# Thirteenth paired unit for the queries and forget gates of heads 4 and 5, bias table and key-value norm moved into the index stage, three attentions beside the branch projection

## The chip, the cores and the metric

One NeuronCore of one Trainium2 chip runs the whole kernel. The metric is device time in microseconds of one execution; three runs give the median. The engines are PE (TensorE, matrix products), DVE (VectorE), ACT (ScalarE), POOL (GpSimd) and SP (SyncE, which here issues nearly all DMAs). Each engine executes its own instructions in the order in which the program emits them, and waits at an instruction until its inputs are there; everything behind it on that engine waits too.

## The reference

One layer on x of shape (1, 512, 2048) in float32. Cut to what matters:

```
h    = rmsnorm(x)
a_q, a_f, a_i, a_g, c_q, c_kv, k_idx, w_idx, b_g, m_a, m_b = split(h @ w_in)
# branch A, 8 heads of 128: gated linear recurrence over chunks
q = silu(a_q) * 128**-0.5 ; f = lb + (1 - lb) * sigmoid(a_f) ; k = 1 - f ; v = a_i
y_a = rmsnorm(recurrence(q, k, log f, v)) * silu(a_g)
# branch B, 8 heads of 128: an indexer picks 128 keys for each query
cq = rmsnorm(c_q);  q = cq @ w_uq;  k, v = rmsnorm(c_kv) @ w_ukv
score = sum_h relu((cq @ w_qidx)_h . layernorm(k_idx)) * w_idx_h, visible keys only
sel = top_k(score, 128)
y_b = softmax(q k[sel] / sqrt(128) + bias_table[t5_bucket(sel - t)]) v[sel] * silu(b_g)
merged = sigmoid(m_a) * (y_a @ w_pa) + sigmoid(m_b) * (y_b @ w_pb)
out = rmsnorm(x + merged @ w_out)
```

## The kernel before

All matrix products are made of three products of float32r halves (`mm3`, lines 76 to 78): high by high, high by low, low by high. So each block of weights that comes in by DMA (`wr`, 128 x 1024 words, 512 KB) is first split into a high half by ACT (`wh`, L72) and a low half by DVE (`wl`, L73). `prep(i)` does that two blocks ahead of the block that PE works on, and issues the loads further ahead.

There are two kinds of projection jobs. A plain job (`feat_job`) makes one product for each block of 128 features, with 512 columns. A paired unit (`pair_job`, `pair_unit`) takes 512 output features and works by the Winograd form of Strassen's rule: seven products of half size where eight would be needed, with 256 columns each, on sums of inputs and of weights made beforehand (`pair_sums`, L145 to L154). A unit is 8 steps of 7 x 2 x 3 = 42 matrix products, 336 in all. Twelve units run one after the other early on: eleven for gates, and one for the queries and forget gates of heads 6 and 7, which it leaves in DRAM (`qf_d`).

The program is written as one list of jobs. Small work is put into generators, one queue ("lane") for each kind: `hgrn` (the recurrence of two heads, `hgrn_gen(p)` for heads 2p and 2p+1), `top` (the selection), `att` (attention of two heads, `att_gen(p)`), `norm`, `misc`, `t5` (the bias table). `pump()` is called between pieces of a projection job, and advances the first generator of each lane by one `yield`. So the order of the instructions on every engine is fixed by hand: by how many pumps lie between one step of a generator and the next. In a plain job over two blocks of features a pump follows each 12 matrix products of 512 columns. `late` is a list of DMA stores and other calls; what is put there is issued by the `flush` two pumps later.

The order of the stages around the change is: the twelve units; `open_branches`, which loads what the later stages need from DRAM; the index stage (eight jobs on `w_qidx`, each two index heads, with the relu'd scores summed into `M`); `end_index`, which starts `hgrn_gen(3)`, `t5_gen` and `norm_gen` of the key-value rank; `ai_job(3)` (values of heads 6, 7); `af_aq(0)`, `ai_job(1)`, `af_aq(1)`, `ai_job(2)` (forget gates and queries as plain jobs, values), with the selection beside them; `uqkv(0)` (queries, keys, values of attention 0); `af_aq(2)` with attention 0 beside it; `uqkv(1)`; a last plain gate job with attention 1 and the recurrence of heads 4, 5; `uqkv(2)`; the branch projection on `w_pa`, eight plain jobs, with attention 2 beside the first four; `uqkv(3)`; attention 3 beside the last four; then `w_pb`, and the output.

`t5_gen` sets `rb` to zero on POOL and loads `rb`, the one-hot table `oh` and `flip`, two pumps later multiplies `rb` by `oh` on PE (L465), stores the differences in DRAM from ACT's queue, reads them back in a skewed pattern, flips them on PE (L478), and stores the bias of each head in DRAM (`bh_d`), again from ACT's queue. `norm_gen` squares `ckv` on ACT, sums the squares on PE (L575, L576 through L81), takes logarithm and exponential on ACT, and scales and splits the two rows.

`att_gen` loads the bias and adds it to the selection mask on POOL (`att_bias`, `MB`), two pumps later makes the scores (`att_scores`: PE, then DVE adds and takes maxima, two pumps later ACT's exponentials and DVE's scaling), three pumps later transposes them on PE (`att_turn`), and two pumps later multiplies by the values (`att_values`).

Of the kernel before, what the change touches and what calls it, by code (L numbers as in the profile page):

```python
# [34 lines left out]
T, D = 512, 2048  # L35
# [7 lines left out]

STILL, MOVED, RANK = 16, 48, 48

# [5 lines left out]
def hybrid_block(ctx, tc, x, norm_w, w_in, lb_table, gnorm_a, q_norm_w, kv_norm_w, w_uq,  # L51
# [50 lines left out]
    cq_d = dram.tile([4, 128, T], F32, name="cq_d")  # L102
    qf_d = dram.tile([2, 2, 128, T], F32, name="qf_d")

# [103 lines left out]

    def feat_job(src, col, ntile, nk, kc, rhs, evac, before=None, width=T, after=None, place=0):
        at = len(specs)  # L210
        n = ntile * 128
        for k in range(0, nk, kc):
            specs.append(([(0, n, src[k * 128:(k + kc) * 128, col:col + n])], kc, n, place))

        def run():
            if before:
                before()
            ps = [mmp.tile([128, T], F32, name="acc")[:, 0:width] for _ in range(ntile)]
            for i in range(nk // kc):
                prep(at + i)  # L220
                wh, wl = halves.pop(at + i)
                for c in range(ntile):
                    for k in range(kc):
                        kk = i * kc + k
                        rh, rl = rhs(kk)
                        s = slice(c * 128, c * 128 + 128)
                        mm3(ps[c], wh[:, k, s], wl[:, k, s], rh, rl, kk == 0, kk == nk - 1)
                    if kk == nk - 1:
                        evac(c, ps[c])
                    if ntile < 4 or c % 2:  # L230
                        pump()
                if after and i in after:
                    after[i]()

        jobs.append(run)
# [197 lines left out]
    def open_branches():  # L433
# [12 lines left out]
        R.i = enter("norms")  # L446
        R.last = [R.i.tile([128, 2, T], F32, name=n) for n in ("hf", "hk", "hq")]
        R.ckv = R.i.tile([128, 2, T], F32, name="ckv")
        for t, src in ((R.last[0], qf_d[1]), (R.last[2], qf_d[0]), (R.ckv, ckv_d)):
            SP.dma_start(t, src.rearrange("f p t -> p f t"))  # L450

    def t5_gen():
# [108 lines left out]
    def norm_gen(raw, n, w, hi, lo):  # L561
# [16 lines left out]
        yield  # L578
        for j in range(n):
            t = R.i.tile([128, T], F32, name="nt", bufs=2)  # L580
            V.scalar_tensor_tensor(t, raw[:, j, :], w[:, j:j + 1], r, op0=OP.mult, op1=OP.mult)
            split(hi[:, j, :], lo[:, j, :], t)
            if j % 2:
                yield

# [66 lines left out]

    def ai_job(p):
# [25 lines left out]
    def af_evac(p):  # L681
        def evac(c, ps):
            if c == 0:
                if p:
                    drain("hgrn")
                hg[p, "f"] = R.h.tile([128, 2, T], F32, name="hf")
                hg[p, "k"] = R.h.tile([128, 2, T], F32, name="hk")
            f, k, h = hg[p, "f"][:, c, :], hg[p, "k"][:, c, :], 2 * p + c
# [5 lines left out]
    def aq_evac(p):  # L694
        def evac(c, ps):
            if c == 0:
                hg[p, "q"] = R.h.tile([128, 2, T], F32, name="hq")
            q = hg[p, "q"][:, c, :]
# [6 lines left out]
    def hgrn_gen(p):  # L705
        f, k, q = R.last if p == 3 else (hg[p, n] for n in "fkq")

        def place(shape, dtype, name, tag):
            pool = R.i if p == 3 and tag in ("hf", "hk", "hq") else R.h
            return pool.tile(shape, dtype, name=name, tag=tag)  # L710

        gate = R.h.tile([128, 2, T], F32, name="hg")
# [5 lines left out]
        qf, kf, tot = (a.rearrange("p c t -> p (c t)") for a in (q, k, f))  # L718
        if p == 3:
            for c in range(2):  # L720
                V.tensor_scalar(f[:, c], f[:, c], oml[:, 6 + c:7 + c], lb[:, 6 + c:7 + c], op0=OP.mult, op1=OP.add)
            V.tensor_scalar(k, f, -1.0, 1.0, op0=OP.mult, op1=OP.add)
# [67 lines left out]
        yield  # L790
        sq = place([128, 2, T], F32, "hk", "hk")
        zs = []
        o = place([128, 2, T], F32, "ho", "hf")
        for c in range(2):
# [8 lines left out]
            yield  # L803
            zs.append((place([128, T], FR, "hzh", ("hkd", "hst")[c]), place([128, T], FR, "hzl", ("hq", "hS")[c])))
            split(*zs[c], sq[:, c])
# [12 lines left out]
        for c in range(2):  # L818
            y = [place([128, T], FR, f"hy{i}", (("hkd", "hst"), ("hq", "hS"))[i][c]) for i in range(2)]
            split(*y, sq[:, c])  # L820
# [127 lines left out]

    def att_gen(p):
        MB = att_bias(2 * p)  # L950
# [9 lines left out]
        yield  # L960
        att_values(p, 0, PT)
        P = yield from att_scores(p, 1, MB)
        yield
        yield
        yield
        PT = att_turn(P)
        yield
        yield
        att_values(p, 1, PT)
# [164 lines left out]
    def end_index():  # L1134
# [4 lines left out]
        R.h = enter("hgrn", side="right")  # L1139
        lanes["hgrn"].append(hgrn_gen(3))  # L1140
        lanes["t5"].append(t5_gen())
        lanes["norm"].append(norm_gen(R.ckv, 2, c_kvw, R.ckh, R.ckl))

    def open_att():
        drain("norm")
        drain("t5")
        leave("norms")
        R.a = enter("att")
# [37 lines left out]
    def end_hgrn():  # L1186
# [4 lines left out]
        R.u = enter("us", side="right")  # L1191
        load_y(R.ya, ya_d, 4, 6)

    gate_job(44, {1: lambda: (take_x(R.ya, 0), load_y(R.ya, ya_d, 0, 4)),
                  3: lambda: (take_x(R.ya, 1), load_y(R.ya, ya_d, 6, 8)),
                  6: end_hgrn, 7: lambda: take_x(R.yb, 2)})
# [3 lines left out]

    uqkv(2)
    jobs.append(lambda: load_y(R.yb, yb_d, 0, 4))

# [292 lines left out]
```

## Time and profile before

| | |
|---|---|
| median of 3 runs | 1380.72 us (1380.17 to 1382.21) |
| profiled execution | 1380.42 us, of which 1378.6 us are the span from its first to its last instruction |
| PE busy | 1357.1 us, 98% |
| DVE busy | 1062.2 us, 77% |
| ACT busy | 625.0 us, 45% |
| POOL busy | 82.6 us, 6% |
| DMA | 201.59 MB, mean 146 GB/s |
| granted TensorE clock | 0.998 of full speed |

Busy time of PE is modelled from pipelined matrix products, whose records overlap, so it hides small waits. The distance from the start of one matrix product to the start of the next is the surer measure: a stage's duration over its count of products. Times in rows count from the start of the span.

### The profile page before, as it was taken

What the parts mean: (1) busy time and instruction counts of PE and PEld (TensorE: products, weight loads), DVE (VectorE), ACT (ScalarE), POOL (GpSimd) and SP (SyncE); (2) the same over time, 40 slices, a digit from 0 to 9 for tenths busy, and PEclk for the clock granted to TensorE, in tenths of its full rate; (3) what the DMA queues carried; (4) which work ended last, traced back from release to release, by engine and by line L of the source; (5) the groups of instructions that cost most, each with busy time, mean ns of one, the idle gap of its engine ahead of it and who ended that gap; (6) DMA issues with size and microseconds to landing.
All of it is one profiled execution on the core that took longest, in us unless ns stands there. A gap on an engine that the chain in (4) does not pass through costs nothing.

```text
span 1378.6 us, 26386 instructions
## 1 busy us (share of the span) xinstructions
PE 1357.1 (98%) x10796; PEld 1250.5 (91%) x10796; DVE 1062.2 (77%) x1744; ACT 625.0 (45%) x986; POOL 82.6 (6%) x85
## 2 busy tenths in 40 slices
PE   8999999999999999999999999999999999999997
PEld 7888999999999999999878889888888888899996
DVE  6796889988888888777759698667555558899856
ACT  5555445545444444466252433543643333454434
POOL 2100000000000000000302012103010100000000
PEclk9999999999999999999999999999999999999999
DMA  6335345544444444443325243344494656643564
GB/s 205 92 102 143 104 142 169 153 138 140 146 144 129 115 140 138 151 151 94 92 79 155 62 139 89 119 126 148 155 314 159 222 161 215 212 147 121 162 205 169
DMA packets 141834, 201.59 MB, mean 146 GB/s; under 512 B 10209, under 2 KB 83602, under 8 KB 141586
## 3 DMA queue, kind: packets, MB, share of 16 engines
q1 hardware_dynamic: 140322, 198.53, 46.4%
q8 instruction: 84, 1.38, 0.4%
q10 hardware_dynamic: 1392, 1.39, 0.3%
q14 instruction: 36, 0.29, 0.1%
HBM read 165.80 MB, written 34.09 MB: 145 GB/s over the span
## 4 chain that ended last, share of the span: by engine, by line
PE 86%; DVE 9%; ACT 2%; issue 1%; DMA 1%; POOL 0%; ACTq 0%; SPq 0%; DVEq 0%; POOLq 0%
PE pp L77 14%; PE pp L76 14%; PE pp L78 14%; PE acc L76 12%; PE acc L78 12%; PE acc L77 12%; DVE wl L73 1%; PE acc L81 1%; PE hl L81 1%; DVE M L648 1%; DVE m L647 1%; PE ho L81 1%; DVE hq L744 1%; PE sc L78 1%; PE sc L76 1%
## 5 line engine op out<-in xcount | busy, mean ns | idle before, releaser
L150 ACT ACTIVATE bh<-wr 128x768 fp32r<-128x768 f32 x120 | 101.5, 846 | 209.4 <-issue 116.7
L72 ACT ACTIVATE wh<-wr 128x1024 fp32r<-128x1024 f32 (+1 forms) x112 | 116.5, 1042 | 166.0 <-PE acc L77 59.1
L73 DVE TENSOR_TENSOR wl<-wr,wh 128x1024 fp32r<-128x1024 f32 (+1 forms) x112 | 137.7, 1230 | 66.2 <-ACT wh L72 66.2
L152 ACT ACTIVATE wh<-sv 128x512 fp32r<-128x512 f32 x240 | 141.9, 622 | 78.3 <-DVE sv L145 60.2
L78 PE MATMUL pp<-sh,wl 128*128 128x256 f32 x576 | 159.5, 277 | 0.0
L76 PE MATMUL pp<-sh,wh 128*128 128x256 f32 x576 | 159.5, 277 | 0.0
L77 PE MATMUL pp<-sl,wh 128*128 128x256 f32 x576 | 159.4, 277 | 0.0
L154 DVE TENSOR_TENSOR wl<-sv,wh 128x1024 fp32r<-128x1024 f32 x120 | 146.7, 1222 | 7.1 <-ACT wh L152 1.1
L153 DVE TENSOR_TENSOR bl<-wr,bh 128x768 fp32r<-128x768 f32 x120 | 114.6, 955 | 48.2 <-ACT bh L150 47.7
L76 PE MATMUL acc<-xh,wh 128*128 128x512 f32 x368 | 148.0, 402 | 0.0
L78 PE MATMUL acc<-xh,wl 128*128 128x512 f32 x368 | 143.8, 391 | 1.5 <-DVE wl L73 1.5
L77 PE MATMUL acc<-xl,wh 128*128 128x512 f32 x368 | 143.4, 390 | 0.0
L77 PEld LDWEIGHTS pp<-sl,wh 128*128 128x128 f32 x576 | 108.3, 188 | 0.0
L78 PEld LDWEIGHTS pp<-sh,wl 128*128 128x128 f32 x576 | 108.3, 188 | 0.0
L76 PEld LDWEIGHTS pp<-sh,wh 128*128 128x128 f32 x576 | 108.3, 188 | 0.0
L76 PE MATMUL pp<-xh,bh 128*128 128x256 f32 x384 | 106.0, 276 | 0.0
L78 PE MATMUL pp<-xh,bl 128*128 128x256 f32 x384 | 106.0, 276 | 0.0
L77 PE MATMUL pp<-xl,bh 128*128 128x256 f32 x384 | 106.0, 276 | 0.0
L76 PE MATMUL acc<-yh,wh 128*128 128x512 f32 x256 | 100.0, 391 | 0.0
L78 PE MATMUL acc<-yh,wl 128*128 128x512 f32 x256 | 99.7, 389 | 0.0
L77 PE MATMUL acc<-yl,wh 128*128 128x512 f32 x256 | 99.7, 389 | 0.0
L145 DVE TENSOR_TENSOR sv<-wr 128x512 f32<-128x512 f32 x120 | 82.3, 686 | 8.6 <-DMA wr<-in_w_in_dram 5.2
(386 smaller groups left out, 3639.3 us busy)
## 6 DMA issues: line engine op xcount, KB each, us to landing
wr<-in_w_in_dram SPq DMA_DIRECT2D x144, 512.0 KB, 3.7
wr<-in_w_out_dram SPq DMA_DIRECT2D x32, 512.0 KB, 3.9
mg<-gate_d SPq DMA_DIRECT2D x48, 256.0 KB, 5.0
gate_d<-c SPq DMA_DIRECT2D x44, 256.0 KB, 4.5
wr<-in_w_pa_dram SPq DMA_DIRECT2D x16, 512.0 KB, 4.1
wr<-in_w_pb_dram SPq DMA_DIRECT2D x16, 512.0 KB, 4.2
wr<-in_w_in_dram SPq DMA_DIRECT2D x20, 256.0 KB, 2.8
x<-in_x_dram SPq DMA_DIRECT2D x8, 512.0 KB, 6.8
```

The source lines that it names most:

```text
L72: A.activation(hi, src, AF.Copy)
L73: V.tensor_tensor(lo, src, hi.bitcast(F32), op=OP.subtract)
L76: PE.matmul(ps, lh, rh, start=first, stop=False, skip_group_check=True)
L77: PE.matmul(ps, lh, rl, start=False, stop=False, skip_group_check=True)
L78: PE.matmul(ps, ll, rh, start=False, stop=last, skip_group_check=True)
L81: PE.matmul(ps, l, r, start=first, stop=last, skip_group_check=True)
L145: V.tensor_tensor(sv[:, 0:2, :], b[:, 1:3, :], b[:, 0:1, :].to_broadcast([128, 2, 256]), op=OP.add)
L150: A.activation(bh, b[:, 1:4, :], AF.Copy)
L152: A.activation(vh[:, i:i + 2, :], sv[:, i:i + 2, :], AF.Copy)
L153: V.tensor_tensor(bl, b[:, 1:4, :], bh.bitcast(F32), op=OP.subtract)
L154: V.tensor_tensor(vl, sv, vh.bitcast(F32), op=OP.subtract)
L647: V.max(m8, m)
```

## The change

It does five things. The queries and forget gates of heads 4 and 5 become a thirteenth paired unit, behind the one for heads 6 and 7; `af_aq(2)` goes away, and the results are read from DRAM (`qf_d` doubles), with scaling done in `hgrn_gen`. The recurrences run in the order 3, 2, 0, 1, with `ai_job(2)` behind `ai_job(3)`. The bias table and the key-value norm start in `open_branches`, beside the index jobs, rather than behind them; the table's stores go through `late` to SP's queue rather than ACT's, with other counts of pumps between its steps. Attention 0 runs beside the last gate job, and attentions 1, 2 and 3 beside the branch projection, which now pumps twice as often (`often`), with one more pump in each rest of those three. And the weights of `w_uq` are put 32 words lower in their buffer (`RANK`).

```
-STILL, MOVED, RANK = 16, 48, 48
+STILL, MOVED, RANK = 16, 48, 16
...
+                        if often and k == 1:
+                            pump()
...
     R.i = enter("norms")
-    R.last = [R.i.tile([128, 2, T], F32, name=n) for n in ("hf", "hk", "hq")]
     R.ckv = R.i.tile([128, 2, T], F32, name="ckv")
-    for t, src in ((R.last[0], qf_d[1]), (R.last[2], qf_d[0]), (R.ckv, ckv_d)):
-        SP.dma_start(t, src.rearrange("f p t -> p f t"))
+    SP.dma_start(R.ckv, ckv_d.rearrange("f p t -> p f t"))
+    for p in (3, 2):
+        for n in "fkq":
+            hg[p, n] = place(p, [128, 2, T], F32, "h" + n, "h" + n)
+        for i, n in enumerate("qf"):
+            SP.dma_start(hg[p, n], qf_d[i, 2 * p - 4:2 * p - 2].rearrange("f p t -> p f t"))
+    lanes["norm"].append(norm_gen(R.ckv, 2, c_kvw, R.ckh, R.ckl))
+    lanes["t5"].append(t5_gen())
...
-    A.dma_start(t5_d, tl)
+    late[1].append(lambda: SP.dma_start(t5_d, tl))
+    yield
+    yield
     yield
     for h in range(0, H, 2):
         if h % 4 == 0:
...
-            for _ in range(4):
-                yield
+            yield
+            yield
...
-        A.dma_start(bh_d[h:h + 2].rearrange("h p c -> p h c"), e)
+        late[1].append(lambda h=h, e=e: SP.dma_start(bh_d[h:h + 2].rearrange("h p c -> p h c"), e))
...
+def place(p, shape, dtype, name, tag):
+    if p == 1 or tag not in ("hf", "hk", "hq"):
+        return R.h.tile(shape, dtype, name=name, tag=tag)
+    return R.i.tile(shape, dtype, name=name, tag=f"{tag}{p or 3}")
...
 def att_gen(p):
+    def rest(n):
+        for _ in range(n + (p > 0)):
+            yield
...
-    yield
-    yield
-    yield
+    yield from rest(3)
     PT = att_turn(P)
-    yield
-    yield
+    yield from rest(2)
     att_values(p, 0, PT)
...
-    if j == 16:
-        pair_job(w_in, [768, 1792], NK // 2, x_pair, pair_evac([qf_d[0], qf_d[1]], [AF.Silu, AF.Sigmoid]))
+    for p in (2, 3) if j == 16 else ():
+        pair_job(w_in, [p * 256, 1024 + p * 256], NK // 2, x_pair,
+                 pair_evac([qf_d[i, 2 * p - 4:2 * p - 2] for i in range(2)], [AF.Silu, AF.Sigmoid]))
...
-    lanes["hgrn"].append(hgrn_gen(3))
-    lanes["t5"].append(t5_gen())
-    lanes["norm"].append(norm_gen(R.ckv, 2, c_kvw, R.ckh, R.ckl))
+    lanes["hgrn"].extend((hgrn_gen(3), hgrn_gen(2)))
...
 ai_job(3)
 lane("top", top_gen)
+ai_job(2)
 af_aq(0)
 ai_job(1)
 af_aq(1)
-ai_job(2)
 jobs.append(open_att)
 uqkv(0)
-af_aq(2)
-uqkv(1)
...
-uqkv(2)
-jobs.append(lambda: load_y(R.yb, yb_d, 0, 4))
+uqkv(1)
+jobs.append(lambda: load_y(R.yb, yb_d, 0, 2))
...
-    feat_job(w_pa, j * 128, 2, H, 4, y_rhs("ya"), pa_evac(j))
-    if j == 6:
-        uqkv(3)
-    if j == 8:
-        jobs.append(lambda: load_y(R.yb, yb_d, 4, 6))
+    feat_job(w_pa, j * 128, 2, H, 4, y_rhs("ya"), pa_evac(j), often=True)
+    if j in (4, 8):
+        uqkv(j // 4 + 1)
+    if j in (6, 10):
+        jobs.append(lambda h=j // 2 - 1: load_y(R.yb, yb_d, h, h + 2))
```

## Rows read from the trace of the kernel before

**Rows 1.** The page: busy time by engine, and the chain that ended last.

```profile
PE 1357.1 (98%) x10796; PEld 1250.5 (91%) x10796; DVE 1062.2 (77%) x1744; ACT 625.0 (45%) x986; POOL 82.6 (6%) x85
...
PE 86%; DVE 9%; ACT 2%; issue 1%; DMA 1%; POOL 0%; ACTq 0%; SPq 0%; DVEq 0%; POOLq 0%
```

**Rows 2.** Windows: length, busy PE, PEld, DVE, ACT, POOL (counts), clock, DMA share, GB/s.

```profile
585.52:646.30 60.78, 59.27 (x338) 56.47 (x337) 45.05 (x74) 37.73 (x75) 1.59 (x4) 1.00 0.39 120
646.30:740.00 93.70, 90.18 (x983) 76.91 (x982) 66.28 (x132) 37.58 (x50) 11.36 (x9) 1.00 0.38 115
1005.00:1134.00 129.00, 129.00 (x632) 109.22 (x631) 68.67 (x139) 43.17 (x76) 11.52 (x16) 1.00 0.63 205
```

**Rows 3.** Window of the twelve paired units, instructions of tile pp alone (no POOL).

```profile
126.19:585.52 459.33, 459.33 (x4032) 459.29 (x4031) 51.24 (x81) 6.95 (x12) 1.00 0.46 138
```

**Rows 4.** Window inside af_aq(2), instructions of tile acc alone.

```profile
869.41:883.03 13.62, 13.62 (x60) 11.08 (x60) 0.00 (x0) 0.00 (x0) 1.00 0.26 72
```

**Rows 5.** Waits of PE, 646 to 740 us: total, times, longest.

```profile
PE hl L81 <- DVE tot L749: 1.6, 1, 1.6
PE acc L78 <- DVE wl L73: 1.5, 1, 1.5
PE hp L81 <- ACT hkd L774: 0.3, 1, 0.3
```

**Rows 6.** Waits of ACT in the same stretch.

```profile
ACT hv L677 <- DVE nt L480: 9.7, 1, 9.7
ACT L515 <- DVE tl L467: 7.5, 1, 7.5
```

**Rows 7.** Timeline of SP's queue from 586 us: start, duration, what.

```profile
591.29 0.49 SPq L450 DMA_DIRECT2D hf<-qf_d  x1
...
592.33 0.47 SPq L450 DMA_DIRECT2D ckv<-ckv_d  x1
593.21 3.32 SPq L128 DMA_DIRECT2D wr<-in_w_qidx_dram  x2
```

**Rows 8.** DMA issues, 586 to 603 us: size, us from issue to landing.

```profile
hf<-qf_d SPq DMA_DIRECT2D x1, 512.0 KB, 4.4
...
ckv<-ckv_d SPq DMA_DIRECT2D x1, 512.0 KB, 7.8
```

**Rows 9.** Timeline of ACT, 589 to 603 us.

```profile
590.21 0.85 ACT L72 ACTIVATE qih<-acc 128x384 fp32r<-128x384 f32 x2
...
601.54 1.06 ACT L72 ACTIVATE wh<-wr 128x1024 fp32r<-128x1024 f32 x1 [0.29 <-DMA wr<-in_w_qidx_dram]
```

**Rows 10.** Timeline of PE at the start of the index stage.

```profile
590.73 0.50 PE L76 MATMUL sc<-kih,qih 128*128 128x512 f32 x1 [0.89 <-ACT qih L72]
...
596.98 0.33 PE L76 MATMUL acc<-cqh,wh 128*128 128x384 f32 x1
```

**Rows 11.** Timeline of POOL, 593 to 595 us.

```profile
594.02 0.34 POOL L445 CAST levels<-lev 128x192 uint8<-128x192 f32 x1 [548.11 <-DMA lev<-in_levels_dram]
```

**Rows 12.** Window over the third head of the index stage.

```profile
596.98:600.65 3.67, 3.67 (x24) 3.54 (x22) 2.23 (x5) 1.79 (x5) 0.00 (x0) 1.00 1.02 346
```

**Rows 13.** Groups of DVE instructions, 646 to 720 us: count, busy us, mean ns, idle before.

```profile
L480 DVE COPY nt<-t 128x512 f32<-128x512 f32 x4 | 2.7, 686 | 0.3 <-PE t L478 0.3
```

**Rows 14.** Attention 2, first head: bias load on SP, mask with bias on POOL.

```profile
1004.37 0.45 SPq L871 DMA_DIRECT2D bh<-bh_d  x1
...
1009.86 2.13 POOL L878 TENSOR_TENSOR MB<-M,bh 128x256 f32<-128x256 f32 x3
```

**Rows 15.** Attention 2, second head: DVE after the values, PE after the scores, DVE's scaling.

```profile
1035.09 0.69 DVE L940 TENSOR_TENSOR ag<-po,ag 128x512 f32<-128x512 f32 x1 [2.49 <-PE po L78]
...
1036.85 0.39 PE L76 MATMUL acc<-yh,wh 128*128 128x512 f32 x1
...
1043.33 1.27 DVE L912 TENSOR_SCALAR P<-P,sm 128x512 f32<-128x512 f32 x4
```

**Rows 16.** Window near the end of the span, behind the last matrix product.

```profile
1373.00:1376.00 3.00, 0.00 (x0) 0.00 (x0) 0.95 (x2) 1.14 (x2) 0.00 (x0) 0.62 0.83 314
```

More of the change, by code (lines that the diff above doesn't have):

```diff
@@ L102, in hybrid_block @@
     cq_d = dram.tile([4, 128, T], F32, name="cq_d")
-    qf_d = dram.tile([2, 2, 128, T], F32, name="qf_d")
+    qf_d = dram.tile([2, 4, 128, T], F32, name="qf_d")
     pools = {}
@@ L207, in hybrid_block, with feat_job @@
     jobs, hg = [], {}
-    def feat_job(src, col, ntile, nk, kc, rhs, evac, before=None, width=T, after=None, place=0):
+    def feat_job(src, col, ntile, nk, kc, rhs, evac, before=None, width=T, after=None, place=0,
+                 often=False):
         at = len(specs)
@@ L578, in norm_gen @@
         yield
[L579 to L583, printed above, removed]
-                yield
+        for j in range(0, n, 2):
+            ts = [R.i.tile([128, T], F32, name="nt", bufs=2) for _ in range(2)]
+            for i, t in enumerate(ts):
+                V.scalar_tensor_tensor(t, raw[:, j + i, :], w[:, j + i:j + i + 1], r, op0=OP.mult, op1=OP.mult)
+            for i, t in enumerate(ts):
+                split(hi[:, j + i, :], lo[:, j + i, :], t)
+            yield
     def kidx_gen():
@@ L683, in evac @@
             if c == 0:
[L684 to L687, printed above, removed]
+                hg[p, "f"] = place(p, [128, 2, T], F32, "hf", "hf")
+                hg[p, "k"] = place(p, [128, 2, T], F32, "hk", "hk")
             f, k, h = hg[p, "f"][:, c, :], hg[p, "k"][:, c, :], 2 * p + c
@@ L696, in evac @@
             if c == 0:
-                hg[p, "q"] = R.h.tile([128, 2, T], F32, name="hq")
+                hg[p, "q"] = place(p, [128, 2, T], F32, "hq", "hq")
             q = hg[p, "q"][:, c, :]
@@ L705, in hgrn_gen @@
     def hgrn_gen(p):
[L706 to L710, printed above, removed]
+        f, k, q = (hg[p, n] for n in "fkq")
         gate = R.h.tile([128, 2, T], F32, name="hg")
@@ L718, in hgrn_gen @@
         qf, kf, tot = (a.rearrange("p c t -> p (c t)") for a in (q, k, f))
-        if p == 3:
+        if p >= 2:
             for c in range(2):
-                V.tensor_scalar(f[:, c], f[:, c], oml[:, 6 + c:7 + c], lb[:, 6 + c:7 + c], op0=OP.mult, op1=OP.add)
+                h = 2 * p + c
+                V.tensor_scalar(f[:, c], f[:, c], oml[:, h:h + 1], lb[:, h:h + 1], op0=OP.mult, op1=OP.add)
             V.tensor_scalar(k, f, -1.0, 1.0, op0=OP.mult, op1=OP.add)
@@ L790, in hgrn_gen @@
         yield
-        sq = place([128, 2, T], F32, "hk", "hk")
+        sq = place(p, [128, 2, T], F32, "hk", "hk")
         zs = []
-        o = place([128, 2, T], F32, "ho", "hf")
+        o = place(p, [128, 2, T], F32, "ho", "hf")
         for c in range(2):
@@ L803, in hgrn_gen @@
             yield
-            zs.append((place([128, T], FR, "hzh", ("hkd", "hst")[c]), place([128, T], FR, "hzl", ("hq", "hS")[c])))
+            zs.append((place(p, [128, T], FR, "hzh", ("hkd", "hst")[c]),
+                       place(p, [128, T], FR, "hzl", ("hq", "hS")[c])))
             split(*zs[c], sq[:, c])
@@ L818, in hgrn_gen @@
         for c in range(2):
-            y = [place([128, T], FR, f"hy{i}", (("hkd", "hst"), ("hq", "hS"))[i][c]) for i in range(2)]
+            y = [place(p, [128, T], FR, f"hy{i}", (("hkd", "hst"), ("hq", "hS"))[i][c]) for i in range(2)]
             split(*y, sq[:, c])
@@ L949, in att_gen @@
     def att_gen(p):
+        def rest(n):
+            for _ in range(n + (p > 0)):
+                yield
         MB = att_bias(2 * p)
@@ L954, in att_gen @@
         MB = att_bias(2 * p + 1)
-        yield
-        yield
-        yield
+        yield from rest(3)
         PT = att_turn(P)
-        yield
-        yield
+        yield from rest(2)
         att_values(p, 0, PT)
         P = yield from att_scores(p, 1, MB)
-        yield
-        yield
-        yield
+        yield from rest(3)
         PT = att_turn(P)
-        yield
-        yield
+        yield from rest(2)
         att_values(p, 1, PT)
@@ L1146, in open_att @@
         drain("t5")
+        while len(lanes["hgrn"]) > 1:
+            for _ in lanes["hgrn"].popleft():
+                pass
+        flush()
+        flush()
         leave("norms")
@@ L1191, in end_hgrn @@
         R.u = enter("us", side="right")
-        load_y(R.ya, ya_d, 4, 6)
-    gate_job(44, {1: lambda: (take_x(R.ya, 0), load_y(R.ya, ya_d, 0, 4)),
-                  3: lambda: (take_x(R.ya, 1), load_y(R.ya, ya_d, 6, 8)),
+        load_y(R.ya, ya_d, 2, 4)
+    gate_job(44, {1: lambda: (take_x(R.ya, 0), load_y(R.ya, ya_d, 0, 2)),
+                  3: lambda: (take_x(R.ya, 1), load_y(R.ya, ya_d, 4, 8)),
                   6: end_hgrn, 7: lambda: take_x(R.yb, 2)})
```

## The prediction

> **What bounds the kernel now.** I read the page first: PE is busy 98% of the span, and 86% of the chain that ended last is PE's [rows 1]. So an edit is worth what it takes out of PE's stream or out of PE's waits; DVE, ACT and the DMAs count only where PE waits for them. Then I cut the span into stages [rows 2] and counted matrix products against time, because busy time of PE hides small waits. In the branch projection PE runs without a gap, and DVE is busy 68.67 of 129.00 us: there is room. In the index stage DVE is busy 45.05 of 60.78 us: there is room too, but less. The stretch 646 to 740 us is the one with waits that can be named [rows 5].
>
> **The unit.** The twelve units take 459.33 us with 4032 matrix products [rows 3]: 459.33 / 12 = 38.28 us each, 0.114 us for a product of 256 columns. In `af_aq(2)` 60 products of 512 columns take 13.62 us [rows 4], 0.227 us each, and it has 2 x 16 x 2 x 3 = 192 of them: 43.6 us. Replacing it by a unit gives 38.3 - 43.6 = -5.3 us. Both figures are of PE at work without waits, so the bounds are close: -5.0 to -5.5. The unit's DVE work (sums and splits) runs beside it as in the other twelve; its extra stores and reads (1 MB each way) come back below.
>
> **The stretch behind the index stage.** Table and norm leave it. What PE waited for there was a product of `tot` (1.6 us), a low half of weights (1.5) and a copy of `hkd` (0.3) [rows 5], 3.4 us in all. Each of the three had ACT or DVE behind it held up: ACT waited 7.5 us for the table's `tl` and 9.7 us for a copy of its `nt` [rows 6], because a store issued from ACT's queue stands in that queue until its data is there, and the splits of weights and the norm's exponential stand behind it. With table and norm gone and the stores on SP, I take all of it: -3.4. Bounds -1.5 (the wait for the low half also has sigmoid and logarithm of two generators ahead of it, which stay) to -3.9.
>
> The Trainium skill ("DMA: Bandwidth & Descriptors", the table's row on spreading DMAs over SP, ACT and GpSimd) says that spreading saves only the sequencer's issue time. By that alone five stores moved from ACT to SP would be worth nothing for PE, and this term would shrink to what the norm's absence gives, 1.6, and the sum below would be 1.8 us higher. Rows 6 show ACT blocked for far longer than an issue, so I stay with the rows.
>
> **The index stage.** This is the step that decides. The first pump after `open_branches` comes behind the first index head's product, and now issues the table's loads; the third pump, two heads later, puts the product of `rb` and `oh` into PE's stream. Before, PE was past the scores of the second head, at that very place, at 596.98 us [rows 10]. PE will have to wait there until `oh` has landed, and everything of PE stands behind it.
>
> When does `oh` land? SP issued the first of the reads in `open_branches` at 591.29 us [rows 7]. Before there were three reads of 512 KB; now there are five (`ckv` first, then two each for heads 6, 7 and 4, 5), then a block of index weights as before, and only then `rb` (which waits for a fill on POOL, behind the cast at 594.02 [rows 11]), `oh` (192 KB) and `flip` (64 KB). The first read landed 4.4 us after issue, at 595.7, the third 7.8 us after issue, at 600.1 [rows 8], and the block of weights was there at 601.54, when ACT's wait for it ended [rows 9]. So after 595.7 there are four more reads, a block and the 256 KB in front, 2.1 + 0.52 + 0.26 = 2.88 MB. At the 346 GB/s that the DMAs moved in those us [rows 12] this takes 8.3 us: 604.0. By the pace of the two reads, (600.1 - 595.7) / 2 = 2.2 us each, it is 595.7 + 4 x 2.2 + 1.4 + 0.7 = 606.6; a little above the rate of those rows, at 390 GB/s, 603.1. I take 604.0, since the bulk rate is what most of the queue goes by: a wait of 604.0 - 596.98 = +7.0 us, bounds +6.1 to +9.6. A gain is excluded here: the product was never waited for before.
>
> Other waits fall inside this one. The norm's squares now stand in ACT's queue between the first two splits (590.21 [rows 9]) and wait for `ckv` until some 595.7 + 1.3; so the second head's scores come about 2 to 3 us late, but the table's product would have kept PE waiting anyway.
>
> Behind that wait the stage still has to hold the rest of table and norm. DVE had 60.78 - 45.05 = 15.7 us free [rows 2]; the table's four copies are 2.7 us at 686 ns [rows 13], and about eight more operations of that size for norm and table make 5.5: 8.2 of 15.7, spread over 14 heads. Logarithm and exponential with their two table loads hold ACT for some 4 us at once, one head's length (3.67 [rows 12]), so a score may wait for a bank. I take +0.7, bounds 0 to +2.5. The products of table and norm on PE only move.
>
> **The branch projection.** A pump comes now after 6 products, 6 x 0.227 = 1.36 us, rather than 2.72. From scores to transposition there are 2 + 3 + 1 = 6 pumps, 8.2 us, where there were five of 2.72, 13.6. What must fit in: in the second head of attention 2 the products by the values ended about 1034.9, DVE's multiplication began at 1035.09, the scores ended at 1036.85, and the last scaling at 1043.33 + 1.27 = 1044.60 [rows 15]. So 7.75 us pass from the end of the scores to the last scaling, with a split of weights among them, and 8.2 are there. The first head of an attention has its mask late: bias load issued at 1004.37, mask ready at 1011.99 [rows 14], while the scores will come 2.7 us earlier than they did; from the mask, maxima, exponentials and scaling need the same time as before, and end about when the transposition is due. Six heads at 0 to 0.7 us each; I take +0.7 in all, bounds 0 to +4. DVE's load is no bound: three attentions at the old rate would be 68.67 x 1.5 = 103 us at most, in about 146 us.
>
> **What costs nothing.** The recurrences in another order are the same work beside the same jobs, each starting when the one before it ends; what hides them is PE's own stream of projection products, and if one of them is late it shows as a wait of `hl` on DVE as now (1.6 in rows 5). Attention 0 beside the last gate job takes the place of attention 1. The branch loads are the same bytes in other portions, and are due 10 us after issue or later. `RANK` moves where 96 products read their weights; I find no row that prices it, and take 0, bounds -0.5 to +0.5 (2% of 96 x 0.23).
>
> **Sum.** -5.3 - 3.4 + 7.0 + 0.7 + 0.7 = -0.3 us on the profiled execution's 1380.42: 1380.1. That execution is 0.3 us below the median of 1380.72, so a median would be 1380.4. About 0.2%, 2.8 us, is what a measurement of this kernel can tell from no change; so this is no change.
>
> **Rivals.**
>
> *The table's loads do not queue behind the big reads.* If small transfers pass the large ones, `oh`, issued near 595, lands 4.4 us later as the first read did, at 599.5: a wait of 2.5 in place of 7.0, and 1375.9. For it: nothing ties the loads together but the engines that move them. Against it: the third read took 7.8 us where the first took 4.4 [rows 8], as if in a line. If the projection also hides all, 1375.
>
> *Closer steps make the transpositions wait.* The place is `att_turn` in attentions 1 to 3; the path of 7.75 us against 8.2 has 0.4 us to spare, and one more split of weights on DVE (1.23 us, about the length of the scaling in rows 15) between maxima and scaling is enough to overrun. If each of the six heads pays 1.2 us it is 7.2 in place of 0.7: 1386.9, slower. It decides from about 0.7 us per head. Against it: the split in rows 15's stretch is already counted in the 7.75, and a second comes only 5.4 us later.
>
> *The clock falls during the wait.* Near the end of the trace, in three us without a matrix product, the granted clock averages 0.62 [rows 16], on its way from 1.00 to 0.5, 2.4 to 1.2 GHz. The new wait leaves PE without work for about 4 us (from 600, when the late scores end, to 604). If the clock fell and stayed down for as long, half of 4 us is lost on top: +2, 1382.4. The Trainium skill ("TensorE: Matmul & The Clock Gate", "HAM oscillation") warns of this for PE waits on DMA in a loop; that row agrees that idleness lowers the clock, and no row shows how fast it returns. Together with the late bound of `oh` this reaches 1385.
>
> *The unit does not pay*, because DVE holds it up: against it, twelve units run at 0.114 us a product; 2 in 100 and not priced apart.
>
> **How the numbers follow.** No change (the wait eats the gain): 0.41. Faster, mostly by the first rival or by a wait nearer 4 us: 0.32. Slower: 0.27, of which closer steps 0.13, the clock and a late `oh` 0.12, the unit 0.02. The likeliest gives 1380.4, its own range 1378 to 1383.3. The range to hold 8 in 10 reaches to the first rival with all hidden, 1375.0, and to 1386.0, near the second.
>
> **What would show it.** Between the old 585.5 and 646.3 (38 us later now) PE waits once, for about 7 us, at L465 for the load of `oh`; if it waits under 4, I am wrong on the queue. The waits on `tot` and `wl` of 646 to 740 us are gone from the list, and ACT waits for `nt` and `tl` no more. Thirteen units take 13 x 38.28 us. In the branch projection transpositions (`tA`) follow products with gaps under 1 us. A granted clock under 1.00 in the index stage would show the third rival. The prediction is wrong if PE's wait at L465 is small, or if waits at `tA` sum to more than 4 us.

## The result, and the profile after

The changed kernel takes 1400.17 us (1399.23 to 1401.02), the one before 1380.45 beside it: a ratio of 1.0141, 95% interval 1.0123 to 1.0158. It is slower by 19.7 us. 1380.4 with 1375.0 to 1386.0 was forecast, no change, so the forecast was wrong, and by more than its range. The profiled execution's span is 1398.7 us. Two of all the executions, one of the kernel before at 4815 us and one with shorter rests at 1428.5 us, are far above the others of their kernels and are left out of the ratios.

The windows of the kernel after, columns as in [rows 2]: the units (tile `pp` alone, no POOL column), the index stage, and the stretch from there to the first product on `w_pa`.

```profile
125.80:623.37 497.57, 497.57 (x4368) 497.53 (x4367) 55.46 (x87) 7.51 (x13) 1.00 0.47 139
623.37:700.91 77.54, 68.76 (x351) 60.64 (x349) 51.55 (x86) 43.44 (x84) 1.60 (x4) 0.93 0.45 137
700.91:1004.17 303.26, 289.81 (x3270) 252.97 (x3269) 230.08 (x431) 116.99 (x170) 53.42 (x42) 0.98 0.37 113
```

Thirteen units take 497.57 / 13 = 38.27 us each, as in [rows 3]. The index stage went from 60.78 us [rows 2] to 77.54, at a mean clock of 0.93. The third stretch shows a clock of 0.98 and 13.5 us without PE (303.26 - 289.81); the same stretch of the kernel before, in its own profile, is the next row: 4.8 us without PE (359.17 - 354.37).

```profile
646.30:1005.47 359.17, 354.37 (x3603) 306.13 (x3601) 264.58 (x508) 150.71 (x225) 58.11 (x50) 1.00 0.39 122
```

PE's waits of the kernel after, from three lists: 623 to 701 us, 700 to 960 us, 1004 to 1140 us. They answer to [rows 5].

```profile
PE sc L76 <- ACT qih L72: 3.7, 2, 2.5
PE t L473 <- DMA oh<-in_buckets_dram: 2.4, 1, 2.4
PE sc L76 <- ACT relu L639: 2.0, 2, 1.9
...
PE hl L81 <- POOL hk L755: 4.4, 2, 4.2
PE hl L81 <- DVE hk L731: 3.8, 1, 3.8
PE hl L81 <- DVE hq L746: 3.8, 2, 2.3
PE hl L81 <- DVE hq L713: 1.4, 2, 0.8
...
PE tA L933 <- DVE P L922: 0.2, 1, 0.2
```

The waits on `tot`, `wl` and `hkd` are gone, as forecast, and the transpositions wait for 0.2 us. New are 13.4 us of waits of `hl`. All but 0.3 of them lie at the seams, where one recurrence follows another: 3.8 us at the first, 7.1 at the second, 2.2 at the third. Behind the longest of them PE runs at half clock; of the windows below (same columns) the first is in the index stage, the second at the first seam, the last two at the second.

```profile
636.59:646.83 10.24, 7.82 (x22) 5.47 (x21) 6.08 (x12) 4.17 (x9) 0.00 (x0) 0.50 0.60 211
766.30:773.13 6.83, 5.33 (x74) 4.43 (x75) 5.70 (x12) 0.14 (x1) 0.00 (x0) 0.50 0.85 255
834.57:837.98 3.41, 3.31 (x74) 3.25 (x75) 3.38 (x8) 0.00 (x0) 0.00 (x0) 0.50 0.96 271
844.80:848.22 3.42, 3.42 (x17) 3.42 (x18) 3.39 (x6) 0.00 (x0) 1.42 (x1) 0.50 0.03 7
```

**The first seam, line by line.** From the timelines of DVE, SP, PE and POOL of the kernel after, 759 to 778 us, put in order of time: heads 6, 7 end and heads 4, 5 begin.

```profile
759.10 0.75 DVE L825 SCALAR_TENSOR_TENSOR hk<-ho,cols,hk 128x512 f32<-128x512 f32 x1 [4.62 <-ACT hk L822]
...
764.80 1.22 DVE L73 TENSOR_TENSOR wl<-wr,wh 128x1024 fp32r<-128x1024 f32 x1
...
766.04 0.37 SPq L128 DMA_DIRECT2D wr<-in_w_in_dram  x1
766.46 0.50 SPq L721 DMA_DIRECT2D hg<-gate_d  x1
...
766.96 0.69 DVE L731 TENSOR_SCALAR hk<-hf 128x1024 f32<-128x1024 f32 x1
767.01 2.81 SPq L832 DMA_DIRECT2D ya_d<-hy  x4
...
767.80 1.08 PE L81 MATMUL hl<-hq,hk 128*32 128x32 f32 x64 [3.77 <-DVE hk L731]
...
774.82 0.96 POOL L725 MEMSET hS<- 128x1024 f32 x1 [39.83 <-DMA ya_d<-hy]
775.75 1.52 POOL L755 TENSOR_TENSOR hk<-hk,hf 128x512 f32<-128x512 f32 x1
...
777.41 0.76 PE L81 MATMUL hl<-hq,hk 128*32 128x32 f32 x64
```

DVE stands for 4.62 us behind the tail's exponential on ACT, and everything of the new recurrence stands behind DVE: the tail's products, the split of a block of weights, and only then the three new operations that scale `hf` and `hk`. PE waits 3.77 us for the last of them. A second chain runs beside it: the tail's last tile shares its buffer with `hS`, the next recurrence fills `hS` with zeros on POOL, and POOL stands there for 39.83 us until the tail's store has landed. SP issues that store only at 767.01, behind a weight load that goes out at 766.04, when DVE's split of that buffer has ended (764.80 + 1.22). POOL's product for `hk`, which the third scores need, comes behind the filling and ends at 775.75 + 1.52 = 777.27; the third scores start at 777.41. At the next seam this chain is the longer one: the wait of 4.2 us in the list.

In the kernel before, a new recurrence began well behind the last one's end. SP's queue there, at the seam from heads 6, 7 to heads 0, 1:

```profile
724.38 3.66 SPq L822 DMA_DIRECT2D ya_d<-hy  x4
736.18 0.50 SPq L713 DMA_DIRECT2D hg<-gate_d  x1
```

The load of `hg` is the first thing that a recurrence issues. It came 11.8 us behind the stores of the recurrence before; in the kernel after it goes out ahead of them (766.46 and 767.01). For the two seams behind that one the kernel before also had a line in the evacuation of the forget gates (`af_evac`) that ran the old recurrence to its end first. The change takes it out:

```
-                if p:
-                    drain("hgrn")
```

**The index stage.** SP, ACT and PE of the kernel after, in order of time; they answer to [rows 7], [rows 9] and [rows 10].

```profile
629.49 0.49 SPq L451 DMA_DIRECT2D ckv<-ckv_d  x1
...
633.98 0.46 SPq L468 DMA_DIRECT2D oh<-in_buckets_dram  x1
...
634.61 1.15 ACT L575 ACTIVATE nsq<-ckv 128x512 f32<-128x512 f32 x2 [5.73 <-DMA ckv<-ckv_d]
...
636.19 0.50 PE L76 MATMUL sc<-kih,qih 128*128 128x512 f32 x1 [2.45 <-ACT qih L72]
...
642.07 1.44 PE L473 MATMUL t<-oh,rb 128*8 128x384 f32 x2 [2.42 <-DMA oh<-in_buckets_dram]
...
645.21 0.53 PE L78 MATMUL acc<-cqh,wl 128*128 128x384 f32 x1
645.53 0.53 PE L76 MATMUL acc<-cqh,wh 128*128 128x384 f32 x1
...
656.32 1.29 ACT L72 ACTIVATE ckh<-nt 128x512 fp32r<-128x512 f32 x2 [2.04 <-DVE nt L592]
```

The stage starts 623.37 - 585.52 = 37.85 us later than before, so without a new wait PE would have come to the table's product at 596.98 + 37.85 = 634.83; it starts at 642.07, 7.24 us late, where 7.0 was forecast. PE stands at the product itself for 2.42 us only. The rest of the 7.24 is in the second head's scores ahead of it, which wait 2.45 us for ACT (the norm's squares, held up by `ckv`, stand ahead of the split of `qih`) and then run at half clock. Not in the sum: the products behind it follow each other every 0.32 us, at half clock, and a later split on ACT, the norm's `ckh`, waits 2.04 us for DVE and holds up a relu for which PE then waits.

### The profile page after: what moved, and what is told of

Same layout as the page of the kernel before. It is cut to its first block, busy times and chain, and to the rows that moved or that the text cites. A ratio compares the mean times of both kernels' runs of the same rounds, so it can differ in the third digit from the quotient of the medians.

```text
span 1398.7 us, 26795 instructions
## 1 busy us (share of the span) xinstructions
PE 1361.7 (97%) x10940; PEld 1258.8 (90%) x10940; DVE 1087.3 (78%) x1780; ACT 632.0 (45%) x1003; POOL 83.1 (6%) x85
## 5 line engine op out<-in xcount | busy, mean ns | idle before, releaser
L152 ACT ACTIVATE wh<-sv 128x512 fp32r<-128x512 f32 x256 | 151.7, 623 | 83.9 <-DVE sv L145 64.9
L78 PE MATMUL pp<-sh,wl 128*128 128x256 f32 x624 | 172.8, 277 | 0.0
L76 PE MATMUL pp<-sh,wh 128*128 128x256 f32 x624 | 172.7, 277 | 0.0
L77 PE MATMUL pp<-sl,wh 128*128 128x256 f32 x624 | 172.7, 277 | 0.0
L73 DVE TENSOR_TENSOR wl<-wr,wh 128x1024 fp32r<-128x1024 f32 (+1 forms) x104 | 125.5, 1207 | 49.6 <-ACT wh L72 49.2
L154 DVE TENSOR_TENSOR wl<-sv,wh 128x1024 fp32r<-128x1024 f32 x128 | 156.5, 1223 | 7.4 <-ACT wh L152 1.1
L76 PE MATMUL acc<-xh,wh 128*128 128x512 f32 x304 | 123.1, 405 | 0.0
L78 PE MATMUL acc<-xh,wl 128*128 128x512 f32 x304 | 119.4, 393 | 0.0
L77 PE MATMUL acc<-xl,wh 128*128 128x512 f32 x304 | 119.2, 392 | 0.0
L77 PEld LDWEIGHTS pp<-sl,wh 128*128 128x128 f32 x624 | 117.3, 188 | 0.0
```

Of the source, the lines that this page charges most:

```text
L73: V.tensor_tensor(lo, src, hi.bitcast(F32), op=OP.subtract)
L76: PE.matmul(ps, lh, rh, start=first, stop=False, skip_group_check=True)
L77: PE.matmul(ps, lh, rl, start=False, stop=False, skip_group_check=True)
L78: PE.matmul(ps, ll, rh, start=False, stop=last, skip_group_check=True)
L152: A.activation(vh[:, i:i + 2, :], sv[:, i:i + 2, :], AF.Copy)
L154: V.tensor_tensor(vl, sv, vh.bitcast(F32), op=OP.subtract)
```

## The experiments

Times are medians beside runs of the kernel before (1379.7 to 1380.5). "After" is 1400.2. Theory A: the loss is at the seams between recurrences, which have no pump to spare any more, and in the index stage. Rivals: DVE is overloaded in the whole stretch (B), or the table's and norm's place explains all (C).

### The seams

**Rest.** Three pumps of rest ahead of the second and the third recurrence.

```
         yield
+        for _ in range(3 if p in (2, 0) else 0):
+            yield
```

> Three more steps of rest at the start of the recurrences of heads 4, 5 and of heads 0, 1; all else as after. Theory A (a recurrence that starts right behind another asks PE for products whose inputs DVE, ACT and POOL still have to make, behind the tail of the one before): the waits of `hl` on `hk` and `hq` near 755 to 774 us and 827 to 849 us go, with the stretches at half clock beside them; these two seams hold some 12 us of waits and 13.7 us at half clock, so 10 to 15 us faster than after: 1385 to 1390. Rival B (DVE and ACT are simply overloaded in this stretch by selection and recurrence together): rest only shifts the waits, 0 to 3 us: 1397 to 1400. Rival C (all of the loss is the table and the norm in the index stage): 1400.

Measured 1387.9, ratio 1.0053 (1.0037 to 1.0070): 12.2 us back. PE's waits behind the index stage, all that are left of 1 us and more:

```profile
PE hl L81 <- DVE hq L713: 2.5, 2, 1.4
PE hl L81 <- DVE hq L755: 1.7, 3, 1.1
PE hl L81 <- DVE hq L748: 1.3, 1, 1.3
```

The waits on `hk` are gone and no stretch between 663 and 1382 us is at half clock. The stretch behind the index stage, to be held against the 303.26 and 289.81 of the kernel after:

```profile
702.02:993.97 291.95, 285.20 (x3270) 247.90 (x3269) 229.22 (x431) 117.03 (x170) 53.19 (x42) 1.00 0.38 118
```

It is 11.3 us shorter: PE stands still for 6.7 us less, and is busy for 4.6 us less with the same 3270 products, which now run at full clock. B falls: DVE's work is the same (229.22 us busy, 230.08 before the edit). C falls: table and norm are where they were.

**Own buffers.** The tail's two tiles that share a buffer with `hS` get one of their own.

```
-                       place(p, [128, T], FR, "hzl", ("hq", "hS")[c])))
+                       place(p, [128, T], FR, "hzl", ("hq", "hS2")[c])))
...
-            y = [place(p, [128, T], FR, f"hy{i}", (("hkd", "hst"), ("hq", "hS"))[i][c]) for i in range(2)]
+            y = [place(p, [128, T], FR, f"hy{i}", (("hkd", "hst"), ("hq", "hS2"))[i][c]) for i in range(2)]
```

> The two tiles of the second head in a recurrence's tail that share a buffer with the state `hS` get a buffer of their own; all else as after. Theory A, in detail: at the seam near 840 us `hl` waits 4.4 us for POOL's `hk`, which stands behind the filling of `hS` with zeros, and that waits until the store of the tail's second tile has landed. Then 4 to 6 us faster than after (the wait, and some of the 3.4 us at half clock next to it): 1394 to 1396. Rival D (POOL's `hk` is late because of its inputs from DVE and ACT, and not because of the buffer): 0 to 1 us, 1399 to 1400.

Measured 1394.4, ratio 1.0102 (1.0087 to 1.0117): 5.8 us back. POOL's product at the second seam starts at 835.93, behind PE and no longer behind a store, where it was 842.42:

```profile
835.93 1.54 POOL L755 TENSOR_TENSOR hk<-hk,hf 128x512 f32<-128x512 f32 x1 [21.67 <-PE hl L81]
```

**Early scaling.** `scale(2)`, the operations on `hf`, `hk`, `hq` of heads 4 and 5, moves into the fifth level of heads 6 and 7, out of the start of their own recurrence.

```
-        if p >= 2:
...
+        if p == 3:
+            scale(3)
...
+            if (p, l) == (3, 4):
+                scale(2)
```

> After, with the scaling of forget gates, keys and queries of heads 4 and 5 done within the recurrence of heads 6 and 7 rather than at the start of its own. Theory A, as to the first seam: PE waits 4.15 us there for `hk`, the last of these operations, and then half clock for 6.8 us. If the operations themselves (three on DVE, 4 us at most) are the delay, 4 to 7 us faster than after: 1393 to 1396. Rival H (the tail of the recurrence before, its logarithm and exponential on ACT and what DVE does behind them, is the delay, whatever stands behind it): 0 to 2 us, 1398 to 1400.

Measured 1403.2, ratio 1.0169 (1.0155 to 1.0182): slower by 3.0, against both expectations; each of its four runs is above each of the four of after. The wait on DVE's `hk` is gone, but PE now waits 7.04 us for POOL:

```profile
776.36 0.95 POOL L733 MEMSET hS<- 128x1024 f32 x1 [41.50 <-DMA ya_d<-hy]
...
778.81 1.08 PE L81 MATMUL hl<-hq,hk 128*32 128x32 f32 x64 [7.04 <-POOL hk L759]
```

So the two chains end close together at the first seam, and taking away the one only shows the other. That asks for both at once, early scaling and own buffers:

> After, with the early scaling of heads 4 and 5 and with the separate buffers, and without any rest. If the early scaling alone lost 3 us because PE then came 7 us too early for POOL's `hk`, which stands behind the filling of `hS` and so behind the landing of the tail's store, then with the separate buffers that wait goes and the early scaling pays: 1394.4 (buffers alone) less 3 to 5, so 1389 to 1392. If the early scaling loses for another reason (its DVE work falls where PE needs DVE more): 1395 to 1398.

Measured 1388.6, ratio 1.0063 (1.0050 to 1.0077): 11.5 us back without any rest, where the parts alone gave -5.8 and +3.0. POOL's product at the first seam now starts at 767.47:

```profile
767.47 1.52 POOL L759 TENSOR_TENSOR hk<-hk,hf 128x512 f32<-128x512 f32 x1 [18.75 <-PE hl L81]
```

Two chains thus hold the seams, DVE's and POOL's; rest hides both, or each can be cut.

**The clock's share.** Idle products in front of the waiting scores keep PE at work.

```
             ps = bank("hl")
+            for _ in range({(2, 0): 15, (0, 1): 8, (0, 2): 16}.get((p, l), 0)):
+                mm(ps, xh[0][:, 0, 0:128], xh[0][:, 0, :], True, True)
```

> After, with idle products put ahead of three of the seams' scores: 15, 8 and 16 products of 512 columns on data that is there, into the bank that the scores overwrite, so that PE works through most of the waits of 4.15, 2.6 and 4.45 us rather than standing idle; the waits themselves are not shortened. Theory A with the clock as a part of the price: the three stretches at half clock near 766, 835 and 845 us (13.7 us in all) go, and with them up to 6.8 us; 4 to 6 us faster than after, 1394 to 1396. Rival G (the clock's fall costs nothing, since DVE and POOL hold PE up anyway): 0 to 1 us, 1399 to 1400.

Measured 1400.7, ratio 1.0151 (1.0137 to 1.0165): nothing back. The granted clock of 763.00 to 773.13 us is 1.00 where it was 0.66 in the kernel after. All three of the scores still wait behind their idle products (0.37, 0.49 and 3.00 us), so these delay nothing. The window in the kernel after, then here:

```profile
763.00:773.13 10.13, 6.37 (x79) 4.97 (x78) 8.97 (x18) 3.44 (x5) 0.00 (x0) 0.66 0.57 172
...
763.00:773.13 10.13, 9.76 (x164) 7.66 (x164) 9.81 (x22) 2.17 (x3) 0.00 (x0) 1.00 0.71 221
```

The first and the third scores of heads 4 and 5 in the timeline of the same kernel:

```profile
766.53 0.75 PE L81 MATMUL hl<-hq,hk 128*32 128x32 f32 x64 [0.37 <-DVE hk L731]
...
776.02 0.76 PE L81 MATMUL hl<-hq,hk 128*32 128x32 f32 x64 [2.15 <-POOL hk L755]
```

Rival G holds: PE comes to the third scores earlier and waits there for POOL, so that they start 9.5 us behind the first ones (776.02 - 766.53), where it was 9.6 (777.41 - 767.80). Taking away half clock alone gives nothing back at these seams; it came back (4.6 us, above) where rest took the waits away with it. The Trainium skill ("TensorE: Matmul & The Clock Gate", "HAM oscillation") books time at half clock as a penalty; by that alone half of the 10.2 us that went from half to full clock (two of the three stretches, 6.83 and 3.41), an estimate of 5 us, would have come back. The measurement, nothing back, decides otherwise for this place.

### The index stage

**Later table.** The table's first product waits three pumps more, the norm starts two later.

```
-        yield
-        yield
+        for _ in range(5):
+            yield
...
     def norm_gen(raw, n, w, hi, lo):
+        yield
+        yield
```

> The table's first product comes three pumps later, and the norm begins two pumps later; still in the index stage. Theory A: the product of `rb` and `oh` finds `oh` landed, the wait of 7.2 us at L473 (with what it covers) goes, and the clock stays at full in the stage but for what the late relu costs; 8 to 11 us faster than after: 1389 to 1392. Rival E (the product only makes visible a delay that the scores have anyway, because DVE and ACT are behind): 0 to 4 us, 1396 to 1400.

Measured 1392.3, ratio 1.0088 (1.0073 to 1.0103): 7.8 us back, a little under theory A's 8 to 11 and above rival E's 0 to 4. The edit moves the table's product and the norm together; "Loads first" below parts them. The stage takes 68.30 us at full clock:

```profile
623.30:691.60 68.30, 64.46 (x350) 58.49 (x349) 51.50 (x86) 43.12 (x84) 1.60 (x4) 1.00 0.47 148
```

**Table and norm back.** Both start in `end_index` again, the stores stay on SP.

> Table and norm start behind the index stage again, as in the kernel before; unit, order of recurrences, closer steps and the stores through SP stay. Theory A: the index stage is back near 61 us from 77.5, of which 4.9 us of matrix products only move; the seams keep their loss and get the table's and the norm's work beside them. 7 to 12 us faster than after: 1388 to 1393. Rival C (all of the loss is the table and the norm in the index stage): 1381 to 1384, the gain of the unit then being hidden by nothing else.

Measured 1392.4, ratio 1.0085 (1.0070 to 1.0100): 7.7 us back. In the profiled execution, of 1389.6 us, the index stage is 61.12 us, the stretch behind it 6.2 us longer than after's 303.26:

```profile
623.06:684.18 61.12, 59.26 (x338) 56.46 (x337) 45.04 (x74) 37.45 (x75) 2.59 (x4) 1.00 0.43 135
684.18:993.62 309.44, 292.55 (x3282) 252.96 (x3281) 236.88 (x443) 123.61 (x179) 53.69 (x42) 0.99 0.38 119
```

Of the 6.2, 3.3 are waits: in this list those of `hl` sum to 16.7 us, for 13.4 in the kernel after. PE is busy for 2.7 us more (292.55 - 289.81), at a clock of 0.99 rather than 0.98, so with less time at half clock. What the products of table and norm cost PE is better read from the two index stages at full clock, 64.46 (later table) - 59.26 = 5.2 us. These only move; what the place in the index stage adds is waits and half clock. And of the three waits in [rows 5] only the one on `tot` is left, 0.9 for 1.6 us, though the table is back in its place; the stores are on SP, and another job stands in the second half of that stretch. Which of the two did it, no run here parts.

**Loads first.** `rb`, `oh` and `flip` are issued ahead of the five reads.

```
+        SP.dma_start(rb[0:32], rel_bias)
+        SP.dma_start(oh, c_buckets)
+        SP.dma_start(flip, c_flip)
         SP.dma_start(R.ident, c_ident)
...
-        SP.dma_start(rb[0:32], rel_bias)
-        SP.dma_start(oh, c_buckets)
-        SP.dma_start(flip, c_flip)
```

> After, with the loads of `rb`, `oh` and `flip` issued at the head of `open_branches`, ahead of the five reads of 512 KB; the product of `rb` and `oh` keeps its place. If `oh` is late because it stands in line behind these reads (the prediction's step), it now lands some 4 to 5 us after an issue near 629 us, before PE comes to the product near 635: the wait at the product goes, and with it what the late scores of the second head don't take over (2 to 3.7 us of the 7.2). 3 to 6 us faster than after: 1394 to 1397. If a load at this place is late whatever stands ahead of it: within 1 us, 1399 to 1401.

Measured 1398.0 (1393.9 to 1400.3), ratio 1.0126 (1.0105 to 1.0147): 2.2 us back by the median, between the two expectations; the two intervals overlap, so the time alone does not tell this kernel from after. The trace does. The wait for `oh` has left the list, and the product starts at 638.83, without a wait of its own:

```profile
638.83 1.45 PE L473 MATMUL t<-oh,rb 128*8 128x384 f32 x2
```

The stage starts at 622.97 here, so without a new wait PE would have come to the product at 634.43, and it is still 638.83 - 634.43 = 4.4 us late: those are the late scores, whose wait is now the first of the stage's list:

```profile
PE sc L76 <- ACT qih L72: 3.9, 2, 2.6
```

So `oh` was late because of what stood ahead of it in the queue, and hidden by its lateness the scores were late too, behind the norm's squares. Taking away the one shows the other. The later table had moved both: its waits of PE on `qih` are 1.2 us, for 3.7 in after.

### Together

**Rest, own buffers and later table.**

> The rest of three steps at two recurrences' start, the separate buffers and the later table together, all else as after. Theory A (two places that lose on their own: the seams between recurrences and the table's wait): the gains of the rest (12.2 us) and of the late table (7.8 us) add, the buffers add 0 to 1 behind the rest, so 1379 to 1381, the time of the kernel before and near the 1380.4 that was forecast. Rival F (the gains share a cause, such as the clock that falls in both): clearly less than the sum, 1383 to 1387.

Measured 1379.4 (11 runs), ratio 0.9998 (0.9989 to 1.0007). The gains of the parts add, so F falls, and the kernel is back at the time before. PE's waits that are left behind the index stage:

```profile
PE hl L81 <- DVE hq L715: 2.5, 2, 1.4
PE hl L81 <- DVE hq L757: 1.3, 2, 1.1
PE hl L81 <- issue: 0.7, 1, 0.7
PE hl L81 <- DVE tot L762: 0.4, 1, 0.4
PE hl L81 <- POOL hk L759: 0.3, 1, 0.3
```

They sum to 5.2 us. The kernel before had 4.7 in the same stretch, 3.4 of them in [rows 5].

**With early scaling, and rest ahead of the fourth recurrence too.**

> The kernel with rest, buffers and late table, with the early scaling of heads 4 and 5 and a rest of 3, 2 and 2 steps ahead of the second, third and fourth recurrence. Theory A: what the rest left (4.8 us of waits near 902 to 909 us ahead of the fourth recurrence, 1.5 us near 784) goes as well; 2 to 4 us faster than the kernel without these two: 1376 to 1379, below the kernel before. If what is left has another cause (DVE and ACT overloaded by selection and recurrence): the same as that kernel, 1379 to 1381.

Measured 1379.3, ratio 0.9995 (0.9986 to 1.0004): the same. The waits of `hl` in its list still sum to 5.4 us; they come back at other levels, with no further gain.

**With the norm back behind the index stage.**

> The kernel with rest, buffers and late table, with the norm of the key-value rank started behind the index stage again, as in the kernel before; the table stays in the index stage. Theory A, second part (in the index stage the norm costs PE by itself: its squares hold up the second head's scores by some 2.6 us, its logarithm and exponential a relu by 1.8 us, which the table's wait had covered): 2 to 4 us faster than that kernel's 1379.4, so 1375.5 to 1377.5 and below the kernel before. Rival I (the norm's logarithm and exponential stall PE as much in the recurrence stretch as here): 1379 to 1380.

Measured 1378.1 (11 runs), ratio 0.9990 (0.9981 to 0.9998): 1.3 us below the kernel with the norm in the index stage, less than expected, and the two intervals overlap. The relu's wait of 1.4 us went; the waits on `qih` and `qil` at the stage's start stayed (1.2 and 0.6), so they are not the norm's. Behind the stage the waits of `hl` sum to 7.1 us in its list, for 5.2, which points to rival I in part: the norm costs PE something there too. It is the fastest version, 1.7 us below the kernel before, less than the 0.2% that a measurement can tell.

**Shorter rests beside the branch projection** (five steps rather than six, on the kernel with all three repairs).

```
-            for _ in range(n + (p > 0)):
+            for _ in range(n):
```

> The kernel with rest, buffers and late table, without the one more step in each rest of attentions 1 to 3. By the working of the prediction 7.75 us must fit between a head's scores and its transposition; 6 steps of 1.36 us gave 8.2 us, 5 steps give 6.8, and each of six heads should wait about 1 us in the transposition and perhaps as much ahead of the values: 5 to 8 us slower than 1379.4, so 1384 to 1387. If the closer steps have more room than that working gave them: within 2 us, 1379 to 1381.

Measured 1380.3, ratio 1.0004 (0.9994 to 1.0014): 0.9 us slower, within the noise, and not the 5 to 8 that the prediction's working gave. The transpositions wait twice, 0.6 us in all:

```profile
PE tA L937 <- DVE P L926: 0.6, 2, 0.4
```

## Why the prediction was wrong

**The step that failed** is the first sentence of "What costs nothing": "The recurrences in another order are the same work beside the same jobs, each starting when the one before it ends; what hides them is PE's own stream of projection products". The work is the same, but the first scores of a recurrence need what DVE, ACT and POOL make at its start, and these were still busy with the tail of the one before. Before, `drain` and the projection of the next queries kept the recurrences apart, 11.8 us and more from the old one's stores to the new one's first load. After, the first seam has its queries read from DRAM, and nothing holds the new recurrence back; at the second the last product for the queries of heads 0, 1 stands on DVE at 828.22, right ahead of the last split of the tail of heads 4, 5 at 828.82. The cover that the sentence names, PE's projection products, is one pump long. The text even says how it would show, as a wait of `hl` on DVE; it was priced at nothing, and it took 12.2 us (rest), or 11.5 (both chains cut).

**The unit** (-5.3): right as to its length, 38.27 us each. No run here puts the plain jobs back beside it, so the gain itself is not measured apart.

**The stretch behind the index stage** (-3.4): the three waits went, but waits of the same kind came in other places. With all three repairs the waits of that stretch sum to 5.2 us, for 4.7 before, so the total gained nothing here.

**The index stage's wait** (+7.0): right in place, size and cause. `oh` was there at 642.07 - 37.85 = 604.2 on the old clock, where 604.0 was forecast, and with the loads first the wait vanishes. But the sign that was named for it failed: "if it waits under 4, I am wrong on the queue". PE waited 2.42 us at the product, and the queue was right all the same. The late scores, put at 2 to 3 us, were 4.4 late and took most of the 7.24 on themselves; so a wait at one instruction is no measure of a landing.

**The rest of that stage** (+0.7): mis-sized. After's stage is 77.54 - 60.78 = 16.8 us longer than before's. 5.2 of that are the products of table and norm, which only moved; 11.6 are lost, where 7.0 + 0.7 were counted. PE stands still for 7.3 us more (8.8, for 1.5 before), and is busy for 4.3 us more than at full clock with the table late (68.76 - 64.46). The 4.3 are the third rival, which came true here: products of 384 columns every 0.32 us rather than every 0.17. The idle time holds a term that the working had looked for elsewhere: the relu's wait of 2.0 us came from the split of the norm's rows, which stood on ACT for DVE (the change also puts both scalings of these rows ahead of both splits), and hardly from logarithm and exponential.

**The branch projection** (+0.7): right within its bounds, 0.2 us of waits. The working left it less room than it has: a step less in each rest cost 0.9 us, no more than the noise, and not 5 to 8.

**The sum.** The miss is 1400.2 - 1380.4 = 19.8 us. The seams are 12.2 of it (rest). The index stage lost 11.6 where 7.7 were counted: 3.9. Behind it 5.2 us of waits are left with all three repairs where 4.7 - 3.4 = 1.3 were due: 3.9 more. The 0.7 of the branch projection was not needed. That makes 19.3; these are readings of different runs, so the sum is an estimate, and what is left of the 19.8 is not told apart.

## What to carry to other kernels

When a change lets one pipelined piece of work start right behind another, price the seam: list what the first product of the new piece needs, and from which engine, and what that engine still owes to the old piece. Follow every buffer that old and new share to its last reader; if that is a store, the new piece waits for a landing and for all that stands ahead of the store in its queue. Where removing one wait makes a kernel slower or changes nothing, a second chain ends close to the first; cut both before judging either.

## What was not expected of the hardware

Taking half clock away gave nothing back where PE was ahead of other engines: over ten microseconds around the first seam the granted clock was 1.00 instead of 0.66, and the time 1400.7 instead of 1400.2. And stores of 256 KB held an engine that has no part in them: POOL stood 39.83 us at a filling, the last 7.8 of them from the issue of the first of the tail's stores at 767.01 on.
